# A two-layer hybrid trunk: sixteen row sums spread over two products, parameter products behind x, three inner tiles by block products

## The chip, the core and the metric

The kernel runs on one core of one Trainium2 chip. The metric is the device time of one execution in microseconds (us); less is better. The core has five engines that run their own instruction lists in order and wait for each other through semaphores: TensorE (PE, matrix products, with its weight loads shown as PEld), VectorE (DVE), ScalarE (ACT), GpSimd (POOL) and SyncE (SP). Here SP issues nearly all loads from memory, POOL issues one stream of them, and ACT and DVE prepare operands for PE.

## What is computed

Two pre-norm residual layers over 512 tokens of width 1024, float32. Layer 0 mixes tokens with a state-space layer (S5), layer 1 with forgetting attention (FoX). Each is followed by a gated feed-forward layer (FFN) of inner width 2816 with a causal convolution of width 3. Every sub-layer is modulated by shift, scale and gate, which come from one conditioning vector `c` through a 1024 x 3072 matrix of its own.

```python
def adaln_params(c, w, b):
    mod = jax.nn.silu(c) @ w + b
    shift, scale, gate = jnp.split(mod, 3, axis=-1)
    ...
def s5_mixer(h, w_in, ...):
    u = h @ w_in
    ...                       # discretise, scan over time, read out: y
    y = jax.nn.gelu(y)
    y = y * jax.nn.sigmoid(y @ w_glu)
    return y @ w_out
def conv_ffn(h, w_up, conv_w, conv_b, w_down):
    a, b = jnp.split(h @ w_up, 2, axis=-1)
    ...                       # a_conv: causal convolution of a, width 3
    return (silu(a_conv) * b) @ w_down
for i in range(2):
    h = h + gate * mixer(modulate(h, ...))
    h = h + gate * conv_ffn(modulate(h, ...))
return rmsnorm(h, final_g)
```

## The kernel before

**Products in split form.** Activations lie with features on the 128 partitions and the 512 tokens along the free axis. A product with a weight matrix is made tile by tile: 128 output features (`m`) from 8 input tiles (`k`). To keep float32 precision in PE's faster format, each operand is split in a high and a low part: ACT copies the raw tile to `w_hi` in the rounded format (L277) and DVE subtracts, `w_lo = raw - w_hi` (L278, `put_parts`). PE then does three matmuls for each k (hi by hi, hi by lo, lo by hi, L294). `product` loads a raw tile on SP's queue, has it split, runs its matmuls and calls `evac`, which empties the PSUM tile. There are five buffers each for `w_hi` and `w_lo`, three for `raw`.

**Opening.** The order of the first stage is written by hand (`manual_schedule`). `s5_params` is a generator that makes the S5 parameters out of many small DVE instructions; each `next(params)` emits the piece up to its next `yield`. The piece after the normalisation constants holds `kr`, `ki` and the first two complex products (`cmul` with n = 1 and n = 2, L876 to L881, six DVE instructions each); behind it stands `ga` (L167, the modulation's scale, whose input PE makes at L157 and L162), and behind that the eight instructions that make `x`, one for each k (tile `a_x`, L1130). PE multiplies the first input weight tile by `x` (L1144), two k at a time, between four steps of a product that makes the shift from the weights `ada_w` (L205).

**S5's last two products.** After the scan, `s5` multiplies by `w_glu` (five tiles are done early, into `gps`; three more with `product`) and then by `w_out`. For each tile m of the first product `glu` takes a sigmoid on ACT (L1278), multiplies it on DVE by y, read back from memory (L1279), and splits the result into `zhi` (ACT) and `zlo` (DVE). The product with `w_out` needs `zhi[k]` and `zlo[k]` for k = 0 to 7 in turn, so the eighth tile, made last, is needed at the end of the first `w_out` tile. That tile's evacuation is `h<-mmp` (L362).

**Row sums in the background.** The modulation parameters of later sub-layers are not made on PE but by DVE as row sums: `ada_units` loads 128 rows of 1024 transposed weights into a room `ada_raw` (a DMA that POOL issues, 512 KB, L233), and DVE multiplies them by the row `c_row` and adds them up (L247). A unit is one such row sum; eight units make one shift, scale or gate of a sub-layer, named (i, t). When a unit has been emitted, its room is loaded again for a later one. Units are emitted where a stage calls `tick`:

```python
def tick(self, n):
    while n and self.bg:
        if next(self.bg[0], None) is None:
            self.bg.pop(0)
        else:
            n -= 1
```

The first tick of a list only starts the loads. Eight units, (1, 2), are emitted in the product with `w_out`, two after each tile but the last two; the FFN of layer 0 emits 32 (three parts of sub-layer 2 and (3, 2)).

**The FFN of layer 0.** 22 inner tiles f, in groups of 4, 4, 5, 4 and 5. Each f makes two up tiles (the branch for the convolution and its gate), applies the convolution and silu, and splits the result into `ghi` and `glo`. From the second group on, f is followed by one or two tiles of the down product of the group before. An inner tile is made in one of two ways. A *plain* one is two calls of the usual product: 48 matmuls of 128 x 512. The other way, `quarters`, is by block products: the 2 x 2 blocks of weights and tokens are combined so that seven products of half-size blocks stand for eight: 84 matmuls of 128 x 256 (L550). For this DVE makes four sums of weight blocks (L518, `sums`), splits three tiles of 1024 columns and one of 512 instead of two of 1024, and adds four PSUM pieces (L518, `nm_t`) with copies that ACT makes (L557, `nm_h`). The tuple `plain` names the inner tiles made the first way: 0, 1, 2, 3, 6, 11 and 17.

From f = 4 on the stage ticks once in `gated` and once behind the down tiles, so two units for each f until the list is empty. While units are there, the down weights are loaded into one single room `rawd`, so the next such load can be issued only when DVE has made the `w_lo` of the one before (L278, `w_lo<-rawd`). DVE, ACT and PE instructions of this stage are put in order by the framework's scheduler; the order it makes is part of the program.

**Values of the attention layer.** `fox_values` (L1366) multiplies with the split weights as the moving operand: 96 matmuls with 272 columns and 288 with 256. `VALUES` is the offset, in float32 elements, at which these split weights lie in their buffers; other users of the buffers take 0 or `ASIDE` (22).

## Time and profile before

| what | value |
|---|---|
| median of 3 runs | 1212.27 us |
| lowest and highest | 1211.45 and 1213.45 us |
| the profiled execution | 1215.46 us |
| its span, first to last instruction | 1213.7 us |
| mean granted TensorE clock | 0.991 of full speed |
| ACT busy | 610.0 us, 50% of the span, 1156 instructions |
| POOL busy | 85.8 us, 7%, 145 instructions |
| DMA | 183.81 MB, mean 151 GB/s |

Busy times are of the profiled execution. A busy PE is not a PE at its peak: matmuls overlap, so the time from one to the next is shorter than the duration shown for one. Where a row says "[2.19 <-DVE a_x L1130]", the engine stood idle for 2.19 us before that work, and what ended the wait was the DVE instruction of line 1130 that writes `a_x`.

### The profile page before, as it was taken

What the parts mean: (1) busy time and instruction counts of PE and PEld (TensorE: products, weight loads), DVE (VectorE), ACT (ScalarE), POOL (GpSimd) and SP (SyncE); (2) the same over time, 40 slices, a digit from 0 to 9 for tenths busy, and PEclk for the clock granted to TensorE, in tenths of its full rate; (3) what the DMA queues carried; (4) which work ended last, traced back from release to release, by engine and by line L of the source; (5) the groups of instructions that cost most, each with busy time, mean ns of one, the idle gap of its engine ahead of it and who ended that gap; (6) DMA issues with size and microseconds to landing.
All of it is one profiled execution on the core that took longest, in us unless ns stands there. A gap on an engine that the chain in (4) does not pass through costs nothing.

```text
span 1213.7 us, 20336 instructions
## 1 busy us (share of the span) xinstructions
PE 1183.8 (98%) x7793; PEld 1015.9 (84%) x7793; DVE 1004.6 (83%) x1872; ACT 610.0 (50%) x1156; POOL 85.8 (7%) x145
## 2 busy tenths in 40 slices
PE   6999999999999999999999999999999999999997
PEld 2566678898988899789899888878989999999987
DVE  7799987689899988899788578876899887888865
ACT  3554565335545453445443565764466554555543
POOL 0000000100000000000000343520000000000000
PEclk9899999999999999999999999999999999999999
DMA  9588787531364544544435453432213332333331
GB/s 356 188 266 258 245 271 253 202 99 53 122 204 156 179 163 155 161 159 130 131 125 194 162 173 134 150 109 88 89 55 111 117 121 84 104 103 109 109 100 70
DMA packets 74513, 183.81 MB, mean 151 GB/s; under 512 B 23232, under 2 KB 25632, under 8 KB 73392
## 3 DMA queue, kind: packets, MB, share of 16 engines
q1 hardware_dynamic: 68367, 161.02, 40.5%
q0 software_dynamic: 5760, 20.97, 5.4%
q8 instruction: 61, 1.00, 0.3%
q10 hardware_dynamic: 288, 0.52, 0.1%
q14 instruction: 37, 0.30, 0.1%
HBM read 175.57 MB, written 6.92 MB: 150 GB/s over the span
## 4 chain that ended last, share of the span: by engine, by line
PE 62%; issue 26%; DVE 4%; DMA 4%; POOL 2%; ACT 1%; SPq 0%; POOLq 0%; DVEq 0%; ACTq 0%
PE mmp L294 25%; PE mmp L550 11%; PE aux L550 4%; PE mmp L1174 3%; PE mmp L1366 3%; PE mmp L1203 2%; PE aux L1505 1%; PE aux L1525 1%; POOL ada_raw L233 1%; PE aux L1065 1%; PE mmp L205 1%; DMA ada_raw<-in_ada_t 1%; PE aux L978 1%; PE aux L1057 1%; DVE w_lo L278 1%
## 5 line engine op out<-in xcount | busy, mean ns | idle before, releaser
L278 DVE TENSOR_TENSOR w_lo<-raw,w_hi 128x1024 fp32r<-128x1024 f32 (+4 forms) x173 | 183.2, 1064 | 37.6 <-ACT w_hi L277 37.1
L277 ACT ACTIVATE w_hi<-raw 128x1024 fp32r<-128x1024 f32 (+4 forms) x173 | 154.8, 905 | 102.0 <-PE mmp L294 44.5
L294 PE MATMUL mmp<-ghi,w_hi 128*128 128x512 f32 (+1 forms) x392 | 145.1, 370 | 0.0
L294 PE MATMUL mmp<-ghi,w_lo 128*128 128x512 f32 (+1 forms) x392 | 144.3, 368 | 0.7 <-DVE w_lo L278 0.5
L294 PE MATMUL mmp<-glo,w_hi 128*128 128x512 f32 (+1 forms) x392 | 144.6, 369 | 0.0
L294 PE MATMUL mmp<-a_hi,w_hi 128*128 128x512 f32 (+1 forms) x376 | 138.4, 371 | 1.5 <-ACT a_hi L433 1.5
L294 PE MATMUL mmp<-a_hi,w_lo 128*128 128x512 f32 (+1 forms) x376 | 136.1, 362 | 0.3 <-DVE w_lo L278 0.3
L294 PE MATMUL mmp<-a_lo,w_hi 128*128 128x512 f32 (+1 forms) x376 | 135.7, 362 | 0.0
L550 PE MATMUL mmp<-w_hi 128*128 128x256 f32 x396 | 109.9, 278 | 3.0 <-ACT nm_h L557 2.5
L550 PE MATMUL mmp<-w_hi,w_lo 128*128 128x256 f32 x396 | 109.7, 278 | 0.7 <-DVE w_lo L278 0.7
L550 PE MATMUL mmp<-w_lo,w_hi 128*128 128x256 f32 x396 | 109.5, 277 | 0.0
L557 ACT ACTIVATE nm_h<-mmp 128x256 f32<-128x256 f32 x99 | 37.2, 381 | 108.3 <-PE mmp L550 108.3
L278 DVE TENSOR_TENSOR w_lo<-sums,w_hi 128x1024 fp32r<-128x1024 f32 x74 | 90.1, 1220 | 0.0
L277 ACT ACTIVATE w_hi<-sums 128x1024 fp32r<-128x1024 f32 x74 | 77.0, 1054 | 25.3 <-DVE sums L518 23.4
L294 PEld LDWEIGHTS mmp<-ghi,w_lo 128*128 128x128 f32 x392 | 74.2, 189 | 13.9 <-DVE w_lo L278 1.4
L294 PEld LDWEIGHTS mmp<-ghi,w_hi 128*128 128x128 f32 x392 | 74.2, 189 | 11.9 <-ACT w_hi L277 0.6
L294 PEld LDWEIGHTS mmp<-glo,w_hi 128*128 128x128 f32 x392 | 74.2, 189 | 11.0
L294 PEld LDWEIGHTS mmp<-a_hi,w_hi 128*128 128x128 f32 x376 | 70.2, 188 | 13.2 <-ACT a_hi L433 1.9
L294 PEld LDWEIGHTS mmp<-a_hi,w_lo 128*128 128x128 f32 x376 | 70.6, 188 | 12.5 <-DVE w_lo L278 1.3
L294 PEld LDWEIGHTS mmp<-a_lo,w_hi 128*128 128x128 f32 x376 | 70.7, 188 | 9.7
L362 DVE SCALAR_TENSOR_TENSOR h<-mmp,par,h 128x512 f32<-128x512 f32 (+1 forms) x100 | 68.1, 683 | 11.8 <-PE mmp L294 11.6
L550 PEld LDWEIGHTS mmp<-w_hi 128*128 128x128 f32 x396 | 74.5, 188 | 3.6 <-ACT nm_h L557 2.9
(319 smaller groups left out, 3082.2 us busy)
## 6 DMA issues: line engine op xcount, KB each, us to landing
raw<-in_w_up SPq DMA_DIRECT2D x88, 512.0 KB, 3.4
raw<-in_ada_w SPq DMA_DIRECT2D x40, 512.0 KB, 6.4
ada_raw<-in_ada_t POOLq DMA_DIRECT2D x40, 512.0 KB, 3.9
nf<-nfd SPq DMA_DIRECT2D x8, 1152.0 KB, 7.8
raw<-in_fox_qk SPq DMA_DIRECT2D x16, 512.0 KB, 3.6
raw<-in_w_down SPq DMA_DIRECT2D x24, 320.0 KB, 3.2
rawd<-in_w_down SPq DMA_DIRECT2D x24, 256.0 KB, 3.3
raw<-in_w_down SPq DMA_DIRECT2D x16, 384.0 KB, 3.4
```

The lines of the kernel that those rows point to most:

```text
L205: self.last_mm = nc.tensor.matmul(ps[32 * qq:32 * qq + 32, :], self.sc32[:, k, :], w[:, q * S:(q + 1) * S], start=(step is steps[0]), stop ...
L233: (nc.gpsimd if late else nc.sync).dma_start(ws[n], src)
L277: nc.scalar.activation(hi, src, AF.Copy)
L278: return nc.vector.tensor_tensor(lo, src, hi.bitcast(F32), ALU.subtract)
L294: self.last_mm = self.nc.tensor.matmul(o, wt, xt[:, cols], start=(k == 0 and n == 0), stop=(k == nk - 1 and n == 2),)
L362: add = self.nc.vector.scalar_tensor_tensor(self.h[:, m, cols], ps, self.par[i][:, 16 + m:17 + m], self.h[:, m, cols], op0=ALU.mult, op1=A ...
L550: self.last_mm = nc.tensor.matmul(o, wt[:, k], xt[:, k], start=(first and k == 0 and n == 0), stop=(k == H - 1 and n == 2), skip_group_che ...
L557: a = nc.scalar.activation(t, o, AF.Copy)
L978: nc.tensor.matmul(ps[:, :, cols], x[:, q, r].rearrange("p c j -> p (c j)"), both[:, :, planes, q, :], start=(r == 0), stop=(r == 1), skip ...
L1174: nc.tensor.matmul(ps, w[m][:, k, :], x[:, k], start=(k == 0), stop=(k == KT - 1))
L1203: nc.tensor.matmul(gps[m], wt, xt[:, k], start=(k == 0 and part == 0 and xt is yhi), stop=(k == KT - 1 and part == 1))
L1366: self.last_mm = nc.tensor.matmul(ps[q, b][:, :n], xt[:, k, tb], wt, start=(k == 0 and i == 0), stop=(k == KT - 1 and i == 2),)
```

## The change

Four edits stand in the diff.

1. `fox_values` puts its split weights at offset 16 instead of 106.
2. `s5_params` yields at two more places, behind `ki` and ahead of the product with n = 2, and the loop that makes `x` takes one piece after its third and one after its sixth tile. The first two complex products are so emitted between the tiles of `x`.
3. The list of units in S5's last two products is longer by the eight of (3, 2), sixteen in all, and has three rooms. It ticks once ahead of the three remaining `w_glu` tiles and then in the products themselves, at every fourth k of both, in place of two ticks after a `w_out` tile. The FFN of layer 0 has 24 units instead of 32.
4. In the FFN of layer 0 the inner tiles 6, 11 and 17 are made by block products.

```diff
+import itertools
...
-ROOM, ASIDE, VALUES = 9 * P, 22, P - 22
+ROOM, ASIDE, VALUES = 9 * P, 22, 16
...
         ki = e.mul(ki, rd, keep("ki"))
+        yield
         w1 = tp.tile([P, L, H], F32, name="s5_w1")
...
         for n in (1, 2, 4):
-            if n == 4:
+            if n > 1:
                 yield
...
                             x[:, k], self.h[:, k], self.ga[i][:, k:k + 1], rb, op0=ALU.mult, op1=ALU.mult
                         )
+                        if k in (2, 5):
+                            next(params)
...
-            self.bg = [self.ada_units(units((1, 2)), rooms=("ada_raw", "ada_raw2"))]
+            self.bg = [self.ada_units(units((1, 2), (3, 2)), rooms=("ada_raw", "ada_raw2", "ada_raw3"))]
+            turn = itertools.count(1)
+
+            def step():
+                if next(turn) % 4 == 0:
+                    self.tick(1)
+
             for m in range(HEAD + 1):
                 glu(m, gps[m], slice(0, S))
-            self.product(self.io["s5_w_glu"], range(HEAD + 1, KT), KT, (yhi, ylo), glu)
             self.tick(1)
+            self.product(self.io["s5_w_glu"], range(HEAD + 1, KT), KT, (yhi, ylo), glu, step=step)
             after, y = nxt
             self.product(
-                self.io["s5_w_out"], range(KT), KT, (zhi, zlo), self.add_residual(i), tail=2, after=after, ticks=2
+                self.io["s5_w_out"], range(KT), KT, (zhi, zlo), self.add_residual(i), tail=2, after=after, step=step
             )
...
-        k.bg = [k.ada_units(units(*((2, t) for t in range(3)), (3, 2)))]
-        x = k.ffn(1, 0, x, k.norm_mod(2), ticks=1, plain=(0, 1, 2, 3, 6, 11, 17))
+        k.bg = [k.ada_units(units(*((2, t) for t in range(3))))]
+        x = k.ffn(1, 0, x, k.norm_mod(2), ticks=1, plain=(0, 1, 2, 3))
```

Three places in DVE's list show what moves. Line numbers of the changed kernel are a few higher.

The opening, DVE, before: the last rows of the complex product with n = 2 (`s_w`, `s_pr`, `s_pi`), then `ga`, then all of `x`.

```order
L878 TENSOR_TENSOR s_pr<-s_w_369,s_w_370 128x2x32
L879 TENSOR_TENSOR s_w_369<-s_pr,s_pi 128x64
L880 TENSOR_TENSOR s_w_370<-s_pi,s_pr 128x64
L881 TENSOR_TENSOR s_pi<-s_w_369,s_w_370 128x2x32
L167 SCALAR_TENSOR_TENSOR ga_96<-aux,rest 128x8
L1130 SCALAR_TENSOR_TENSOR a_x<-h,ga_96,aux 128x512 x8
L876 TENSOR_TENSOR s_w_369<-s_pr 128x128
```

The same place of the changed kernel:

```order
L702 TENSOR_TENSOR s_ki<-s_ring_180 128x32
L168 SCALAR_TENSOR_TENSOR ga_96<-aux,rest 128x8
L1132 SCALAR_TENSOR_TENSOR a_x<-h,ga_96,aux 128x512 x3
L878 TENSOR_TENSOR s_w_381<-s_pr 128x32
L879 TENSOR_TENSOR s_w_382<-s_pi 128x32
L880 TENSOR_TENSOR s_pr<-s_w_381,s_w_382 128x32
L881 TENSOR_TENSOR s_w_381<-s_pr,s_pi 128x32
L882 TENSOR_TENSOR s_w_382<-s_pi,s_pr 128x32
L883 TENSOR_TENSOR s_pi<-s_w_381,s_w_382 128x32
L1132 SCALAR_TENSOR_TENSOR a_x<-h,ga_96,aux 128x512 x3
```

Twelve small instructions that stood ahead of `ga` and `x` now stand between the tiles of `x`, six after the third and six after the sixth.

The end of the product with `w_glu`, DVE, before: `w_lo` are split weights for the tiles to come, `nm_t<-nm_t,yt` is the multiplication by y, and the last three rows are the eighth tile of z and the evacuation of the first `w_out` tile.

```order
L278 TENSOR_TENSOR w_lo<-raw,w_hi 128x1024
L1279 TENSOR_TENSOR nm_t<-nm_t,yt 128x8x64
L278 TENSOR_TENSOR zlo<-nm_t,zhi 128x512
L278 TENSOR_TENSOR w_lo<-raw,w_hi 128x1024
L1279 TENSOR_TENSOR nm_t<-nm_t,yt 128x8x64
L278 TENSOR_TENSOR zlo<-nm_t,zhi 128x512
L362 SCALAR_TENSOR_TENSOR h<-mmp,par_92,h 128x512
```

The same place of the changed kernel, from the last two row sums ahead of the eighth tile on:

```order
L248 ISA ada_raw,ada_s<-ada_raw,c_row 128x1024
L248 ISA ada_s 128x1
L248 ISA ada_raw_2090,ada_s<-ada_raw_2090,c_row 128x1024
L248 ISA ada_s 128x1
L279 TENSOR_TENSOR w_lo<-raw,w_hi 128x1024
L1283 TENSOR_TENSOR nm_t<-nm_t,yt 128x8x64
L255 TENSOR_TENSOR par_93<-ada_s,rest 128x8
L279 TENSOR_TENSOR w_lo<-raw,w_hi 128x1024
L279 TENSOR_TENSOR zlo<-nm_t,zhi 128x512
L279 TENSOR_TENSOR w_lo<-raw,w_hi 128x1024 x2
L1283 TENSOR_TENSOR nm_t<-nm_t,yt 128x8x64
L279 TENSOR_TENSOR zlo<-nm_t,zhi 128x512
```

Of the eight row sums that now stand ahead of the first `h<-mmp`, three come before the first multiplication by y and five between the tiles of z; the last two splits of weights, which before stood on both sides of the seventh tile's `zlo`, now follow each other ahead of the eighth.

In the FFN of layer 0, the fourth group, DVE, before: from one use of the single room `rawd` to the next.

```order
L278 TENSOR_TENSOR w_lo<-rawd,w_hi 128x640
L518 TENSOR_TENSOR sums<-raw 128x512 x2
L518 TENSOR_TENSOR nm_t<-aux,nm_h 128x256
L518 TENSOR_TENSOR sums<-sums,raw 128x512
L518 TENSOR_TENSOR sums<-raw,sums 128x512
L518 TENSOR_TENSOR nm_t<-mmp,nm_h 128x256
L278 TENSOR_TENSOR w_lo<-rawd,w_hi 128x640
```

The same place of the changed kernel:

```order
L279 TENSOR_TENSOR w_lo<-rawd,w_hi 128x640
L519 TENSOR_TENSOR sums<-raw 128x512 x2
L519 TENSOR_TENSOR sums<-sums,raw 128x512
L519 TENSOR_TENSOR nm_t<-mmp,nm_h 128x256
L519 TENSOR_TENSOR sums<-raw,sums 128x512
L603 SCALAR_TENSOR_TENSOR conv<-nm_t,conv_wb,conv 128x511
L279 TENSOR_TENSOR w_lo<-raw,w_hi 128x512
L603 SCALAR_TENSOR_TENSOR conv<-nm_t,conv_wb,conv 128x510
L248 ISA ada_raw,ada_s<-ada_raw,c_row 128x1024
L248 ISA ada_s 128x1
L519 TENSOR_TENSOR nm_t<-mmp,nm_h 128x256 x2
L279 TENSOR_TENSOR w_lo<-rawd,w_hi 128x640
```

The scheduler has put the two convolution steps, a split, a row sum and two additions between the two uses of the room, where before the second use followed directly.

## The prediction

> **What bounds the kernel now.** The page's first part and the head of its chain come first; columns are busy time, share of the span and instructions.
>
> ```profile
> PE 1183.8 (98%) x7793; PEld 1015.9 (84%) x7793; DVE 1004.6 (83%) x1872; ACT 610.0 (50%) x1156; POOL 85.8 (7%) x145
> ...
> PE 62%; issue 26%; DVE 4%; DMA 4%; POOL 2%; ACT 1%; SPq 0%; POOLq 0%; DVEq 0%; ACTq 0%
> ```
>
> PE sets the time: its own work and its issue make 88% of the chain. DVE is the one engine near it. So an edit can gain by fewer matmuls or by shorter waits of PE, and it can lose by making DVE late. The view of waits (engine, line, for whom: total us, times, longest) names PE's waits; each starts where DVE or ACT is late.
>
> ```profile
> PE mmp L550 <- ACT nm_h L557: 2.5, 1, 2.5
> PE mmp L1144 <- DVE a_x L1130: 2.2, 1, 2.2
> ...
> PE mmp L550 <- DVE w_lo L278: 1.6, 2, 0.9
> ```
>
> These totals are small because records of matmuls overlap. What a matmul really takes is read in the chain's pieces (start, us, what) where PE runs freely, in the second FFN.
>
> ```profile
> 951.57 8.18 PE mmp L294 x36
> ...
> 962.49 1.36 PE aux L550 x12
> ```
>
> 8.18 / 36 = 0.227 us for 512 columns, 1.36 / 12 = 0.113 for 256. With these I count out the first FFN in three stretches: inner tiles 4 to 12, 13 to 16 and 17 to 21 (up to the last down product). The windows give for each: length, busy us of PE, PEld, DVE, ACT and POOL with their instructions, clock, DMA share, GB/s.
>
> ```profile
> 305.29:439.63 134.34, 133.55 (x876) 121.07 (x875) 123.52 (x194) 65.99 (x106) 8.45 (x16) 1.00 0.53 170
> 439.63:507.87 68.24, 66.52 (x458) 60.74 (x457) 56.18 (x89) 30.69 (x51) 4.24 (x8) 1.00 0.44 145
> 507.87:579.21 71.34, 68.00 (x457) 62.33 (x456) 64.67 (x100) 32.50 (x54) 3.69 (x7) 0.98 0.47 151
> 351.51:405.56 54.05, 53.26 (x398) 49.76 (x396) 51.29 (x82) 27.41 (x46) 3.70 (x7) 1.00 0.51 167
> ```
>
> The 876 matmuls of the first are 588 of 256 columns (7 block tiles) and 288 of 512 (2 plain tiles, 16 down tiles): 588 x 0.1135 + 288 x 0.2272 = 132.2 us, so PE lost **2.2**. In the second, 336 and 120 make 65.4: lost **2.8**. In the third, 336 and 120 again: lost **5.9**. These 10.9 us and the matmuls themselves are what the change can win here.
>
> **The change, part by part. Three block tiles.** PE: a plain tile is 48 x 0.2272 = 10.9 us, a block tile 84 x 0.1135 = 9.5. Three of them: **-4.1**, two in the first stretch, one in the third. DVE pays; its price from one start to the next is read where two equal instructions stand together (start, us, engine, line, operation, tiles):
>
> ```profile
> 298.92 2.35 DVE L278 TENSOR_TENSOR w_lo<-raw,w_hi 128x1024 fp32r<-128x1024 f32 x2
> ...
> 315.22 0.75 DVE L518 TENSOR_TENSOR nm_t<-mmp,nm_h 128x256 f32<-128x256 f32 x2
> ...
> 339.67 1.29 DVE L518 TENSOR_TENSOR sums<-raw 128x512 f32<-128x512 f32 x2
> ```
>
> A second one adds 1.14, 0.33 and 0.60 us. A block tile needs 4 sums of blocks (2.4), one split of 1024 more (1.14), one of 512 (0.6) and 4 additions (1.3) more than a plain one: 5.5 us. In all a block tile is 10.3 us of DVE: sums 2.4, splits 3 x 1.14 + 0.6, additions 1.3, and 2.5 for the four instructions of 512 columns (two convolution steps, the gate, `glo`) that a plain tile has too; a plain tile is 4.8, a down tile 1.3 (a split and `h`), a row sum 1.14. Tiles 4 to 12 with 16 down tiles and 17 row sums are then 121 us (the window shows 123.5 busy, ends of instructions included) and go to 132, while PE's falls to 129.4. DVE becomes the longer one by 2.8 us over nine tiles. The fourth window shows such a stretch: tiles 7 to 10, all by blocks, hold 55.5 us of DVE work by the same prices against 51.8 of PE, an excess of 3.7, and PE lost 2.2 there; 1.5 was carried by work made ahead or left for later, in the plain tiles 6 and 11. Of an excess of 2.8, 1.3 would be left; for waits of DVE itself I add 1.7 and take 3.0 lost after (2.2 before).
>
> **Eight row sums fewer in this FFN.** The list now ends with tile 16, so one row sum of 1.14 us leaves the second stretch and seven, 8 us, the third. The third's DVE work is 64.7 - 8 + 5.5 = 62.2 busy against PE's 64.0, the second's 55 against 65.4. What loses time there, though, is the single room `rawd`: the tile view shows who waited for its load, and two rows show one place.
>
> ```profile
>   ACT w_hi L277: 33.0, 14
>   DVE w_lo L278: 13.5, 7
> ...
> 527.90 0.63 ACT L277 ACTIVATE w_hi<-rawd 128x512 fp32r<-128x512 f32 x1 [3.57 <-DMA rawd<-in_w_down]
> 528.44 0.64 ACT L557 ACTIVATE nm_h<-mmp 128x256 f32<-128x256 f32 x2
> ```
>
> ACT stands 3.57 us for the load, and behind it in ACT's list stand the copies for which PE waits its 2.5 us. It comes when two uses of the room lie close on DVE. By the prices above the work between the uses of one tile was 3.1, 3.1, 3.1 and 0.7 us in tiles 13 to 16, and is 5.3, 5.9, 6.5 and 3.1 now; in the last group two pairs stay at 2.8. So I take 1.0 lost in the second stretch (2.8 before) and 2.0 in the third (5.9). Losses together 6.0 instead of 10.9: **-4.9**. The ends of what is lost: 1.3 (DVE's excess alone) and 19 (with the second rival below).
>
> **Row sums in S5's last products.** Sixteen sums instead of eight; eight stand ahead of the first `w_out` evacuation.
>
> ```profile
> 179.59 0.47 SPq L1270 DMA_DIRECT2D c_row<-scd  x1
> ...
> 183.74 1.18 DVE L1192 TENSOR_TENSOR a_lo<-yt,a_hi 128x512 fp32r<-128x512 f32 x1 [0.83 <-ACT a_hi L1191]
> 190.44 1.23 DVE L278 TENSOR_TENSOR w_lo<-raw,w_hi 128x1024 fp32r<-128x1024 f32 x1 [5.52 <-ACT w_hi L277]
> ...
> 214.22 1.23 DVE L278 TENSOR_TENSOR w_lo<-raw,w_hi 128x1024 fp32r<-128x1024 f32 x1 [1.73 <-ACT w_hi L277]
> 215.36 1.16 DVE L1279 TENSOR_TENSOR nm_t<-nm_t,yt 128x512 f32<-128x512 f32 x1
> 217.22 0.69 DVE L278 TENSOR_TENSOR zlo<-nm_t,zhi 128x512 fp32r<-128x512 f32 x1 [0.70 <-ACT zhi L277]
> 218.82 0.75 DVE L362 SCALAR_TENSOR_TENSOR h<-mmp,par,h 128x512 f32<-128x512 f32 x1 [0.90 <-PE mmp L294]
> ...
> 190.44:214.22 23.78, 23.78 (x111) 19.86 (x110) 20.23 (x23) 14.89 (x23) 0.00 (x0) 1.00 0.72 223
> ...
> DMA to landing us min/median/max: 6.7/6.7/6.7
> ```
>
> Three sums fall in DVE's gap of 5.52 us: `c_row` is there at 179.6 + 6.7 = 186.3 (the landing row is its own), three times 1.14 end at 189.7, and the next split starts at 190.4 as before. The other five, 5.7 us, join 20.2 us of work in 23.8: they need 25.9, so what started at 214.22 starts 2.2 later, and the eighth tile of z with it. PE used that tile within 0.3 us of its being made (`zlo` ends at 217.9, three matmuls of 0.227 end the tile at 218.8). Cost **+1.9**; behind the waiting matmul stand all later ones, so nothing hides it. Ends: 0, if the sums fall in the waits for `zhi` too, and +5.7, if no gap serves. The eight sums behind it stood there before too, with two rooms and waits for their loads; three rooms can only shorten these, and PE did not wait there: 0. POOL issues nothing else there; SP keeps its loads' kinds and count.
>
> **Parameters behind x.**
>
> ```profile
> 19.47 0.37 SPq L186 DMA_DIRECT2D raw<-in_s_w_in  x1
> ...
> 22.54 1.03 PE L162 MATMUL aux<-sel,ada_rows 128*128 128x2 f32 x8
> 27.03 2.71 PE L1144 MATMUL mmp<-a_x,raw 128*128 128x512 f32 x4 [2.19 <-DVE a_x L1130]
> ...
> 26.04 0.16 DVE L167 SCALAR_TENSOR_TENSOR ga<-aux,rest 128x8 f32<-128x8 f32 x1
> ...
> DMA to landing us min/median/max: 5.5/7.9/10.2
> ...
> 43.36 9.55 PE mmp L1174 x16
> 52.91 2.19 PE aux L978 x16
> ```
>
> `ga` could run when PE ends L162, at 23.6; twelve small instructions hold it until 26.0. Now it goes at once, 2.4 us earlier. The first input weights land at 19.47 + 5.5 = 25.0 (the landing row is of the two `s_w_in` loads), so PE starts at 25.0 instead of 27.03: **-2.0**. The later tiles of `x` come 1.3 us apart from the small products, still ahead of PE's pairs. From there to 55 the chain is PE's own work but for 0.2 us, and the scan's first products follow it, so I keep all of it. Ends: 0, if a load or DVE takes it back, and -2.4, all by which `ga` is earlier.
>
> **The offset of the values.**
>
> ```profile
> 641.87 23.93 PE mmp L1366 x198
> ...
> 959.75 2.74 PE mmp L550 x24
> ```
>
> At offset 106 a 256-column matmul of `fox_values` takes 0.121 us, elsewhere 0.114. No trace shows offset 16. Over 288 matmuls the ends are -2.1 (as elsewhere) and +2.1 (as far the other way). This is the one 256-column kind off the common row, so I take half the way to it: **-1.0**.
>
> **Sum.** -4.1 - 4.9 + 1.9 - 2.0 - 1.0 = -10.1. The profiled execution took 1215.5 us around its span of 1213.7, which makes 1205.4; the median of the runs shown lies 3.2 below that execution: 1212.3 - 10.1 = **1202.2 us**.
>
> **Rivals.**
> *The losses in the FFN stay.* DVE's excess early takes the place of the waits on `rawd`. For it: ACT still waits in order for that room. Against: the longer distances. The 4.9 fall away: 1207.1.
> *DVE becomes the bound, and it gets slower.* In tiles 4 to 12 each block tile with two row sums needs 15.1 us of DVE (10.3, two down tiles 2.5, sums 2.3) where PE needs 9.5 + 5.5 = 15.0; with one down tile 13.8 against 12.3. DVE then has no spare for any wait of its own. In the third stretch it was busy 64.7 of 71.3, 91%; at that share 132 us need 145.6 instead of my 132.4, 13.2 more: 1215.4. It decides from the point where DVE's own waits in these nine tiles pass the 3 us that I allow. Against: the fourth window, where DVE was busy 51.3 of 54.05, 95%, and PE lost 2.2.
> *The sums come on the path in S5.* Loads of the rooms run late and DVE stands in front of the splits: +5.7 instead of 1.9 is 1206.0. The Trainium skill, "Trainium Kernel Development and Optimization", section Key Constraints, says that DMAs issued from SP, ACT and POOL queues run on the same 16 DMA engines and interleave; by it SP's weight loads give way to POOL's eight more. The window above has those engines at 0.72.
> *The clock.* The wait before 27.03 goes, and with it perhaps the slow clock behind it:
>
> ```profile
> 27.03:30.20 3.17, 3.17 (x8) 0.88 (x12) 3.17 (x6) 0.00 (x0) 0.00 (x0) 0.68 1.03 420
> ```
>
> Granted 0.68 of full, 3.17 us lose 1.0; with later dips perhaps 2 more: 1199. The Trainium skill, "TensorE: Matmul & The Clock Gate", section What's actually happening, has PE's clock fall to half after an idle window of about 3.4 us, in windows that run free of the kernel; the dip behind a wait of 2.2 us and little work agrees as far as it goes.
>
> **How the numbers follow.** Forecast 42 in 100; losses stay 14; sums on the path 11; clock 7; the second and third together, about 1211, 10; DVE the bound 16, of which 2 within the bounds of no change. About 0.2%, 2.4 us, is what a measurement of this kernel can tell from no change. Faster 0.42 + 0.14 + 0.11 + 0.07 = 0.74, same 0.12, slower 0.14. The range takes the clock's case and the best ends of the offset and the FFN below, 1196, and the two rivals together with the offset's bad end above, 1213.5; it leaves out DVE as the bound and a little below.
>
> **What would show it.** Right: `ga` near 23.7 and PE's first L1144 near 25.0; a wait of PE for `zhi` or `zlo` of about 2 us near the first `w_out` tile; tiles 4 to 12 in 132 to 133 us, 13 to 16 in 66 to 67, 17 to 21 in 66; L1366 at 0.114 to 0.121 us. Wrong: tiles 4 to 12 at 140 or more with DVE at 97%; `w_hi<-rawd` still waiting 3 us ahead of `nm_h`; L1174 ending where it did, at 52.9.

## The result, and the profile after

The change makes the kernel slower. The median of five runs is 1226.4 us (1223.1 to 1230.1) against 1212.8 us (1211.5 to 1215.8) for the kernel before, timed alongside it; the ratio is 1.0109, with a 95% interval of 1.0084 to 1.0134. The profiled execution spans 1222.0 us, 8.3 more than the one before; it is one of the faster ones of the changed kernel, and the one before is among the slower of its kind, so the profiles show a smaller difference than the medians. The last section comes back to a part of this.

The page of the changed kernel, first part (busy time, share of the span, instructions) and head of the chain that ended last:

```profile
PE 1183.5 (97%) x7901; PEld 1018.8 (83%) x7901; DVE 1022.3 (84%) x1902; ACT 618.7 (51%) x1174; POOL 86.3 (7%) x145
...
PE 66%; DVE 14%; DMA 9%; issue 7%; ACT 2%; SPq 0%; POOL 0%; DVEq 0%; ACTq 0%; POOLq 0%
```

PE is as busy as before, but DVE's share of the chain is 14% where it was 4%, and DMA's 9% where it was 4%. So work of DVE and loads now stand on the path. The view of PE's waits (engine, line, for whom: total us, times, longest) says where:

```profile
PE mmp L295 <- ACT zhi L278: 5.7, 1, 5.7
...
PE mmp L295 <- DVE w_lo L279: 5.1, 6, 1.8
PE aux L381 <- DVE ssq L357: 3.8, 2, 3.5
PE mmp L295 <- ACT w_hi L278: 2.1, 1, 2.1
```

The first row is one wait, in S5's last products, and there was none for `zhi` before. The second and fourth are down products of the first FFN. The windows (length, busy us of PE, PEld, DVE, ACT and POOL with their instructions, clock, DMA share, GB/s) give the stages: first the stretch from the start of `w_glu` to the first FFN's norm before, then the same after, then the three stretches of the first FFN after.

```profile
195.69:255.63 59.94, 59.69 (x309) 51.00 (x308) 44.95 (x69) 23.32 (x33) 3.69 (x7) 1.00 0.60 197
```

```profile
189.80:257.67 67.87, 61.90 (x309) 51.95 (x308) 51.81 (x82) 24.42 (x34) 5.81 (x11) 0.95 0.61 213
...
307.61:444.71 137.10, 132.69 (x939) 121.66 (x937) 127.73 (x202) 68.16 (x114) 7.93 (x15) 0.99 0.48 156
444.71:520.99 76.28, 71.32 (x467) 64.10 (x467) 67.88 (x108) 35.72 (x57) 4.22 (x8) 0.98 0.47 156
520.99:585.12 64.13, 64.13 (x493) 61.23 (x492) 56.40 (x87) 34.48 (x59) 0.00 (x0) 1.00 0.33 96
```

| stretch | before, us | after, us | difference | predicted |
|---|---|---|---|---|
| start to S5's scan (first product L978, now L980) | 52.75 | 46.25 | -6.5 | -2.0 |
| scan, to `w_glu` | 142.9 | 143.5 | +0.6 | 0 |
| `w_glu` and `w_out`, to the norm | 59.9 | 67.9 | +7.9 | +1.9 |
| norm, and inner tiles 0 to 3 | 49.7 | 49.9 | +0.3 | 0 |
| inner tiles 4 to 12 | 134.3 | 137.1 | +2.8 | -1.9 |
| 13 to 16 | 68.2 | 76.3 | +8.0 | -1.8 |
| 17 to 21 | 71.3 | 64.1 | -7.2 | -5.3 |
| the last down products, to `fox_values` | 38.1 | 41.3 | +3.2 | 0 |
| `fox_values` | 48.4 | 47.6 | -0.8 | -1.0 |
| the rest | 537.7 | 537.7 | 0.0 | 0 |

Three places lose: S5's last products, the middle of the FFN, and the FFN's end.

**S5's last products.** The chain of work that ended last, in order of time (start, us, what), runs there through four engines and one load:

```profile
205.08 1.21 DVE ada_raw L248
...
206.31 1.14 DVE ada_raw L248
...
207.45 1.15 DVE w_lo L279
...
208.65 5.30 DMA raw<-in_s_w_out
...
214.03 1.06 ACT w_hi L278
...
216.26 1.08 DVE nm_t L1283
...
217.37 0.64 ACT zhi L278
...
218.05 4.15 PE mmp L295 x9
```

Two row sums stand ahead of a `w_lo`. That `w_lo` frees a room of raw weights, so SP can issue the next load only at 208.65. The load takes 5.30 us. ACT's row for its copy shows how it waits for such loads, and what stands behind the copy:

```profile
209.24 1.06 ACT L278 ACTIVATE w_hi<-raw 128x1024 fp32r<-128x1024 f32 x1 [4.66 <-DMA raw<-in_s_w_out]
...
214.03 1.06 ACT L278 ACTIVATE w_hi<-raw 128x1024 fp32r<-128x1024 f32 x1 [3.21 <-DMA raw<-in_s_w_out]
214.99 0.58 ACT L1282 ACTIVATE nm_t<-mmp 128x512 f32<-128x512 f32 x1
```

The row at 214.99 is the sigmoid of the eighth tile. Its input was ready long before, but it is behind `w_hi` in ACT's list, and `w_hi` is of a weight tile that PE needs only later. PE stands 5.7 us for the eighth `zhi`, and its granted clock (the last figure but two) is at about half when it goes on:

```profile
218.05:221.81 3.76, 3.76 (x9) 2.70 (x10) 2.44 (x3) 1.69 (x2) 0.00 (x0) 0.52 0.25 101
```

3.76 us at 0.52 lose 1.8, so the wait and the slow clock behind it make 7.5 of the 7.9 us.

**The first FFN.** DVE's waits in tiles 13 to 17, by line, then two rows of its timeline:

```profile
DVE sums L519 <- DMA raw<-in_w_up: 4.4, 2, 2.3
DVE w_lo L279 <- ACT w_hi L278: 1.5, 1, 1.5
```

```profile
440.51 0.69 DVE L519 TENSOR_TENSOR sums<-raw 128x512 f32<-128x512 f32 x1 [2.06 <-DMA raw<-in_w_up]
...
458.63 0.69 DVE L519 TENSOR_TENSOR sums<-raw 128x512 f32<-128x512 f32 x1 [2.26 <-DMA raw<-in_w_up]
```

In the kernel before DVE never waited for a load of `w_up` in these tiles: it made `sums` and splits ahead, and its waits were for ACT. SP's issues of the two loads of a tile (start, us from the first to the end of the second), before and after, show what changed:

```profile
451.26 10.03 SPq L186 DMA_DIRECT2D raw<-in_w_up  x2
```

```profile
435.56 0.90 SPq L187 DMA_DIRECT2D raw<-in_w_up  x2
```

Before, the first load went out 10.0 us ahead of the second in two of the pairs between 400 and 490 us, and 1.4 to 7.6 us ahead in the other three; after, four of five pairs went out within 0.9 us. The waits of SP's queue in tiles 4 to 16 name what it stood for, after and then before:

```profile
SPq L187 <- DVE sums L519: 44.3, 7, 9.1
```

```profile
SPq L186 <- DVE sums L518: 4.5, 1, 4.5
```

Now DVE reads the raw tiles for `sums` so late that SP issues both loads together, and DVE stands over 2 us for them three times, at 440, 458 and 476 us. The engine that is late makes its own next wait.

### The profile page after: what moved, and what is told of

Same layout as the page of the kernel before. It is cut to its first block, busy times and chain, and to the rows that moved or that the text cites. A ratio compares the mean times of both kernels' runs of the same rounds, so it can differ in the third digit from the quotient of the medians.

```text
span 1222.0 us, 20601 instructions
## 1 busy us (share of the span) xinstructions
PE 1183.5 (97%) x7901; PEld 1018.8 (83%) x7901; DVE 1022.3 (84%) x1902; ACT 618.7 (51%) x1174; POOL 86.3 (7%) x145
## 4 chain that ended last, share of the span: by engine, by line
PE 66%; DVE 14%; DMA 9%; issue 7%; ACT 2%; SPq 0%; POOL 0%; DVEq 0%; ACTq 0%; POOLq 0%
PE mmp L295 33%; PE mmp L551 13%; PE aux L551 5%; DVE w_lo L279 3%; PE mmp L1178 3%; PE mmp L1376 2%; PE aux L1515 1%; PE aux L1535 1%; DVE ada_raw L248 1%; DMA raw<-in_w_up 1%; DMA rawd<-in_w_down 1%; DMA raw<-in_s_w_glu 1%; DVE sums L519 1%; PE aux L1059 1%; PE aux L980 1%
## 5 line engine op out<-in xcount | busy, mean ns | idle before, releaser
L295 PE MATMUL mmp<-a_hi,w_hi 128*128 128x512 f32 (+1 forms) x328 | 119.9, 369 | 1.5 <-ACT a_hi L434 1.5
L551 PE MATMUL mmp<-w_hi 128*128 128x256 f32 x432 | 119.6, 277 | 1.2 <-ACT w_hi L278 1.0
L551 PE MATMUL mmp<-w_hi,w_lo 128*128 128x256 f32 x432 | 119.1, 277 | 0.4 <-DVE w_lo L279 0.4
L551 PE MATMUL mmp<-w_lo,w_hi 128*128 128x256 f32 x432 | 119.3, 276 | 0.0
L295 PE MATMUL mmp<-a_hi,w_lo 128*128 128x512 f32 (+1 forms) x328 | 117.6, 359 | 0.0
L295 PE MATMUL mmp<-a_lo,w_hi 128*128 128x512 f32 (+1 forms) x328 | 117.3, 359 | 0.0
L279 DVE TENSOR_TENSOR w_lo<-sums,w_hi 128x1024 fp32r<-128x1024 f32 x80 | 97.4, 1220 | 0.2 <-ACT w_hi L278 0.2
L551 PEld LDWEIGHTS mmp<-w_hi,w_lo 128*128 128x128 f32 x432 | 80.9, 188 | 0.9 <-DVE w_lo L279 0.7
L551 PEld LDWEIGHTS mmp<-w_lo,w_hi 128*128 128x128 f32 x432 | 81.1, 188 | 0.0
L551 PE MATMUL mmp<-a_hi,w_lo 128*128 128x256 f32 x288 | 80.4, 279 | 0.6 <-DVE w_lo L279 0.5
```

The lines of the kernel that those rows point to most:

```text
L279: return nc.vector.tensor_tensor(lo, src, hi.bitcast(F32), ALU.subtract)
L295: self.last_mm = self.nc.tensor.matmul(o, wt, xt[:, cols], start=(k == 0 and n == 0), stop=(k == nk - 1 and n == 2),)
L551: self.last_mm = nc.tensor.matmul(o, wt[:, k], xt[:, k], start=(first and k == 0 and n == 0), stop=(k == H - 1 and n == 2), skip_group_che ...
```

## The experiments

Ratios are of the runs of each kernel to runs of the kernel before on the same chip, with 95% intervals. "The S5 stretch" is the one from `w_glu` to the norm (59.9 us before, 67.9 after); "the FFN stretch" is inner tiles 4 to 21 (273.9 before, 277.5 after; their matmuls alone, at 0.2272 and 0.1135 us each, take 263.0 before and 258.8 after).

### One edit undone, or alone

The moved row sums undone:

```diff
-units((1, 2), (3, 2)), rooms=("ada_raw", "ada_raw2", "ada_raw3")
+units((1, 2)), rooms=("ada_raw", "ada_raw2")
...
-tail=2, after=after, step=step
+tail=2, after=after, ticks=2
...
-units(*((2, t) for t in range(3)))
+units(*((2, t) for t in range(3)), (3, 2))
```

> The changed kernel with the sixteen row sums put back where they were: eight in S5's last product, 32 in the first FFN (offset, opening and three block tiles stay). Theory (each edit pays by its own stage): the stretch from the start of w_glu to the first FFN's norm, 67.9 us in the changed kernel and 59.9 before, is back at 60; tiles 4 to 21 of the first FFN, 277.5 us in the changed kernel, get eight row sums (9.1 us of DVE) more while DVE is already the late engine, so 283 to 287; total 1226.4 - 7.9 + 5 to 9 = 1224 to 1228. Rival (the FFN's stalls come from S5's delay being carried on, not from the blocks): tiles 4 to 21 fall to about 267, total near 1208.

Measured: 1215.9 us, ratio 1.0026 (1.0009 to 1.0043). The S5 stretch is back at 59.9. The FFN stretch is 280.4, 3 more than in the changed kernel. So the moved sums cost 8 us where they went and gave back 3 where they came from. The total is 8 us under the 1224 to 1228 that I expected: tiles 4 to 21 lost less than the 5 to 9 us that I had put down, and the stretch behind them took 36.2 us instead of 41.3.

The three block tiles undone:

```diff
-x = k.ffn(1, 0, x, k.norm_mod(2), ticks=1, plain=(0, 1, 2, 3))
+x = k.ffn(1, 0, x, k.norm_mod(2), ticks=1, plain=(0, 1, 2, 3, 6, 11, 17))
```

> The changed kernel with tiles 6, 11 and 17 as plain products again (offset, opening and moved row sums stay). Theory (the blocks put DVE behind its loads in the first FFN): tiles 4 to 21 go from 277.5 to 264 to 268 us (their matmuls alone need 263), the S5 stretch stays at 67 to 68, total 1226.4 - 10 to 13 = 1213 to 1217, no change against before. Rival (the moved sums' loads and SP's order make the stalls, the blocks only shift them): tiles 4 to 21 stay at 274 or more, total 1223 or more.

Measured: 1215.9 us, ratio 1.0041 (1.0021 to 1.0061). The FFN stretch falls to 270.5 us, not to the 264 to 268 that I expected, and the S5 stretch is 70.4. Either edit without the other still makes a kernel slower than the one before, by 0.3 to 0.4%.

The opening alone, and the opening with the offset, on the kernel before (the diffs are the first lines of the change's):

> The kernel before with the parameter products behind x alone. Theory (the wait of 2.2 us at the first input product and the half clock behind it are one loss): first scan product near 46 to 47 us instead of 52.75, total 1212.5 - 5 to 6.5 = 1206 to 1207.5. As predicted at first, without the clock: -2.0, 1210.5. Rival (the start of the program differed by chance and DVE takes the rest back in the scan): 1212.

> The kernel before with the parameter products behind x and the offset 16 of the values. Theory: 288 matmuls at 0.117 instead of 0.120 us, 0.8 us less than with the opening alone, 1205 to 1207. Rival (the pitch follows the clock, not the offset): the same time as with the opening alone and a pitch of 0.120.

Measured: 1210.2 us, 0.9985 (0.9968 to 1.0003), and 1208.9 us, 0.9985 (0.9967 to 1.0004). My expectation of -5 to -6.5 us was wrong. The first, -2.0, lies in the interval, and so does no change. The trace shows its mechanism: with the opening alone PE's first input product starts at 24.9 instead of 27.0. Most of the 6.5 us between the two profiles was not won by this edit; the last section comes back to it. The offset moves the middle of the matmul's pitch in `fox_values` from 0.120 us to 0.118, which is 0.6 us over 288 matmuls. The times don't separate it.

### What the row sums cost in S5: VectorE's time or their loads

Two kernels, each the changed one with one half left out in S5's list alone. In the first, the sums after the third run over rooms already loaded, so thirteen loads are left out:

```diff
+                if not loads and n >= len(rooms):
+                    ws[n] = kept[n % len(rooms)]
+                    return
```

> The changed kernel; in S5's list of sixteen row sums the first three rooms are loaded and every later sum is taken over a room already loaded, so thirteen of POOL's sixteen loads there are left out (and with them part of the conditioning's values). Stretch from w_glu's start to the first FFN's norm: 67.9 us in the changed kernel, 59.9 before. Theory A (VectorE's 1.2 us per sum in front of the weight splits is the cost): stays at 66 to 68. Theory B (POOL's loads slow the weights' loads on the shared DMA engines, and ACT stands for them): falls to 60 to 62. Both half: 63 to 65.

In the second, all loads stay and a sum has 16 columns, `full` being false for this list:

```diff
+                cols_ = D if full else 16
...
-                    w, w, self.c_row, 1.0, 0.0, ALU.mult, ALU.add, sums[:, j:j + 1]
+                    w[:, :cols_], w[:, :cols_], self.c_row[:, :cols_], 1.0, 0.0, ALU.mult, ALU.add, sums[:, j:j + 1]
```

> The changed kernel; in S5's list each of the sixteen row sums runs over 16 columns instead of 1024 (the rest of each sum is left out), while all sixteen loads stay. Same stretch: Theory A (VectorE's time): falls to 60 to 62. Theory B (the loads): stays at 66 to 68. Both half: 63 to 65.

Measured: 1218.9 us, 1.0058 (1.0025 to 1.0090), without the loads, and 1224.1 us, 1.0103 (1.0065 to 1.0141), with the loads and hardly any sums. The windows of the S5 stretch, the kernel with sums and no loads first, then the one with loads and hardly any sums:

```profile
190.55:252.80 62.25, 60.21 (x310) 50.95 (x308) 50.23 (x80) 23.36 (x33) 0.00 (x0) 1.00 0.41 135
```

```profile
189.20:256.20 67.00, 63.26 (x310) 52.62 (x308) 40.36 (x82) 25.71 (x36) 5.25 (x10) 0.95 0.61 217
```

DVE's time alone costs 62.2 - 59.9 = 2.3 us, close to the 1.9 that I had put down. The loads alone cost 7.1 us, with DVE only 40 us busy: there PE stands 3.5 us for `zhi` and `zlo`, and its clock is 0.50 from 215.6 to 221.2, which loses 2.8 more. In the full change sums and loads together cost 7.9, not 9.4: the two overlap. So without the loads most of the loss is gone.

How do they cost it? The view of DMA issues (KB each, median us from issue to landing) shows the weights' loads between 195 and 222 us in the kernel before, then in the one with the loads, and between 195 and 218 us in the changed kernel:

```profile
raw<-in_s_w_out SPq DMA_DIRECT2D x7, 512.0 KB, 4.6
```

```profile
ada_raw<-in_ada_t POOLq DMA_DIRECT2D x6, 512.0 KB, 6.6
raw<-in_s_w_out SPq DMA_DIRECT2D x5, 512.0 KB, 7.4
```

```profile
raw<-in_s_w_out SPq DMA_DIRECT2D x6, 512.0 KB, 4.3
```

The Trainium skill, "DMA: Bandwidth & Descriptors", section Issuing engines are not separate DMA queues, says that loads issued from different engines run on the same 16 DMA engines and interleave. 7.4 us instead of 4.6 in the kernel with the loads agrees. But these slower loads are not what PE waited for: ACT stands only 1.2 us for these loads there, and in the changed kernel their median is no longer than before. What stands on the path is single loads. In the kernel with the loads and hardly any sums the chain goes through a row sum's load and, later, through one of y:

```profile
181.04 5.68 DMA ada_raw<-in_ada_t
...
201.29 8.50 DMA yt<-s_yd
```

Loads of y took 3.6 us on the median before. The row sum's load shows as a wait of DVE in list order, from 180 to 222 us of the same kernel (total, times, longest); the wait of 5.8 us is ahead of the first multiplication by y:

```profile
DVE ada_raw L249 <- DMA ada_raw<-in_ada_t: 6.9, 2, 5.8
```

In the changed kernel the load on the chain is the fifth of `w_out`. Without POOL's loads it goes out 16.3 us into the stretch and takes 3.5 us; in the changed kernel it goes out at 18.9 and takes 5.3. So the loads cost by a later issue, behind a later DVE, and by one slower landing; the runs don't divide the loss further.

### The sums later: all sixteen in `w_out`

If the loads of `w_glu` were what they collide with, it would help to emit them after it. Kernel before, with opening and offset, and:

```diff
-units((1, 2)), rooms=("ada_raw", "ada_raw2")
+units((1, 2), (3, 2)), rooms=("ada_raw", "ada_raw2")
...
-tail=2, after=after, ticks=2
+tail=2, after=after, ticks=3
```

(and (3, 2) taken from the FFN's list).

> The kernel before with the parameter products behind x, the offset 16, and all sixteen row sums of S5's list in the w_out product (three per tile, two rooms, none during w_glu); the first FFN has 24. Theory B (in w_glu the sums' loads meet the weights' loads; in w_out the weights are loaded ahead): the stretch from w_glu's start to the norm stays at 60 to 62 us, the FFN's tiles gain 3 us as in no_blocks, total 1209 - 1 to 3 = 1206 to 1208. Rival (anywhere in S5 the sums are on the path): the stretch takes 65 or more, total 1212 or more.

Measured: 1222.1 us, 1.0070 (1.0045 to 1.0095). A miss. The eighth tile of z is in time now, but PE waits at the norm behind `w_out`. Its waits in this kernel:

```profile
PE aux L380 <- DVE ssq L356: 7.3, 3, 5.1
...
PE aux L410 <- DVE rs_y L401: 4.8, 3, 4.4
```

The S5 stretch is 74.2 us. DVE waits 0.2 to 0.8 us for the load of nearly each sum, and the sums of squares for the norm stand behind them. With two rooms for the down weights and tile 17 by block products added, it stays there: 1220.6 us, 1.0063 (1.0038 to 1.0088), more than 10 us above either range that I had put down.

> late_sums with two rooms for the down weights and tile 17 by block products: both gains of the two theories together, 1209 - 2 - 6 - 1.4, 1198 to 1203. If the sums are on the path in w_out: 1204 to 1210.

So neither place in these products had 9 us to spare.

### The single room for down weights

The changed kernel with two rooms, and to make place for the second an unused stretch of memory in this stage, the filler, 128 bytes shorter:

```diff
-            t = self.bgpool.tile(shape, F32, name=self.room, bufs=1)
+            t = self.bgpool.tile(shape, F32, name=self.room, bufs=2)
```

> The changed kernel with two rooms for the down weights in the first FFN instead of one (128 bytes less of the filler there). Tiles 4 to 21 took 277.5 us in the changed kernel, their matmuls 259. Theory C (the single room: SyncE stands in its list until VectorE frees it, so the next loads of w_up come late and two at once): VectorE's waits for w_up's loads (7.0 us in 4 times) go and the stretch falls to 264 to 268, total 1226.4 - 10 = 1216. Theory D (the three rooms of w_up's weights, freed late by VectorE, are the limit): 274 or more, total 1223 or more.

Measured: 1217.1 us, 1.0063 (1.0033 to 1.0093); the FFN stretch is 272.8, not the 264 to 268 expected. DVE's waits for `w_up` fall from 7.0 to 3.3 us. ACT no longer waits for `rawd`. But a block tile where PE runs freely takes 9.83 us here instead of 9.54, for a reason found below.

Four rooms for raw weights instead of three:

> The changed kernel with four rooms for raw weights instead of three (in both FFNs and everywhere else; the filler in the FFNs is 64 bytes instead of 1696). Theory D (three rooms are the limit in the first FFN): tiles 4 to 21 fall from 277.5 to 264 to 268 us, and ACT's waits for w_out's weights in S5 shrink, so that stretch falls from 67.9 to 62 to 65; total 1226.4 - 12 to 16 = 1210 to 1214. Theory C (the single down room) or E (VectorE's amount of work alone, 252 us of it in 277): 274 or more in the FFN.

Measured: 1236.7 us, 1.0212 (1.0175 to 1.0250), 10 us worse than the change. The FFN stretch is some 280 us, not the 264 to 268 of theory D. It tells little of rooms, since the shorter filler moved the tiles of both FFNs: in the second FFN, where nothing waits, 24 matmuls of 256 columns take 2.82 us, against 2.72 in the changed kernel. DVE's waits for `w_up` are gone in the first FFN, as theory D has it, but the time is not; the S5 stretch, 66.3, hardly moved.

Two rooms on the kernel before with opening and offset, its 32 sums and plain tiles kept; and the same with tile 17 by block products:

> The kernel before with the parameter products behind x, the offset 16 and two rooms for the down weights in the first FFN; its 32 row sums and plain tiles stay. Theory C (the single room is what made the stalls of the kernel before too): tiles 4 to 21 fall from 274 us towards their matmuls' 263, by 4 to 8 us, total 1209 - 4 to 8 = 1201 to 1205. Rival (the second room only helps where VectorE is overloaded by blocks): no change against 1209.

> As open_off_rawd2, and tile 17 by block products (6 and 11 stay plain). Theory (there VectorE is not late, so the block's 1.4 us of TensorE are won): 1.4 us under open_off_rawd2. Rival (32 row sums plus a block put VectorE behind at 17 as well): 1 to 3 us over it.

Measured: 1204.8 us, 0.9927 (0.9904 to 0.9950), and 1207.7 us, 0.9956 (0.9939 to 0.9972). In the first PE has no gap above 0.4 us left between tile 4 and tile 21, so nearly all of the 10.9 us that the kernel before lost there was the room's. One block tile more costs 2.9 us where its matmuls are 1.4 us shorter.

### The pitch, and the blocks and sums apart

The filler shortened by 512 bytes instead of 128, first on the kernel with opening, offset and two rooms, then with the three block tiles, then with the whole change:

```diff
-            fill(pool, 1696 - (128 if ticks else 0))
+            fill(pool, 1696 - (512 if ticks else 0))
```

> open_off_rawd2 with the filler of the first FFN shortened by 512 bytes instead of 128. Theory F (the place of the moving operand in steps of 512 bytes sets the matmul's pitch): a block tile is back from 9.83 to 9.54 us, a down tile of 24 matmuls from 5.60 to 5.47, 4 to 21 in 264 to 265 instead of 269; total 1204.8 - 4 to 5 = 1200 to 1201. Rival (the pitch has another reason): 9.83 stays, 1204 to 1206.

> open_off_rawd2_512 with tiles 6, 11 and 17 by block products. Theory G (with two rooms VectorE's amount of work still binds: 32 row sums and three blocks more are 16.5 us more than in the kernel before): 2 to 6 us slower than open_off_rawd2_512, VectorE over 96% busy from tile 6 on, TensorE waiting for w_lo<-sums. Theory H (the rooms were all of it): 3 to 4 us faster, as the matmuls' count says.

> The whole change with two rooms for the down weights and the filler 512 bytes shorter. By theories B and G: S5's stretch 67 to 70 us (8 to 10 more than before), the FFN's tiles 4 to 21 in 262 to 266 with eight row sums fewer than in three_blocks_rawd2_512; total about 1212 to 1216, level with the kernel before. Rival (what S5 loses the FFN regains): within 2 us of three_blocks_rawd2_512 and under 1206.

One block tile without a wait, with 128 and then with 512 bytes:

```profile
453.28:463.11 9.83, 9.83 (x86) 9.83 (x84) 8.81 (x14) 5.06 (x9) 0.53 (x1) 1.00 0.52 180
```

```profile
451.97:461.51 9.54, 9.54 (x86) 9.54 (x84) 9.32 (x15) 4.99 (x8) 0.53 (x1) 1.00 0.56 187
```

Measured: 1199.7 us, 0.9883 (0.9861 to 0.9905), the fastest kernel of the study; 1207.9 us, 0.9954 (0.9936 to 0.9973), with the three block tiles; 1216.2 us, 1.0025 (1.0005 to 1.0046), with the moved sums too. The blocks cost 8.2 us, more than the 2 to 6 that I expected, and the sums 8.3, with two rooms and an undisturbed pitch (the time from one matmul to the next); with the whole change the S5 stretch takes 68.8 us and the FFN stretch 270.3. The FFN stretch of the first two:

```profile
302.85:566.51 263.66, 263.38 (x1789) 242.35 (x1787) 244.75 (x383) 132.43 (x210) 16.38 (x31) 1.00 0.50 165
```

```profile
299.11:572.61 273.50, 265.77 (x1896) 247.70 (x1895) 260.43 (x412) 139.75 (x228) 16.37 (x31) 0.99 0.47 158
```

In the first, PE's matmuls need 263.0 us and take 263.7: nothing is left to win there by waits. DVE has 244.8 us of work, 93%. The blocks add 15.7 us to DVE, 260.4, more than the 258.8 that PE's matmuls now need. So DVE is the longer one, and its own waits come on top. In the worst tiles of this kernel it works nearly all the time:

```profile
400.02:417.50 17.48, 15.22 (x106) 13.85 (x105) 17.05 (x29) 8.05 (x15) 1.58 (x3) 1.00 0.46 155
...
405.26 0.39 PE L550 MATMUL mmp<-w_hi,w_lo 128*128 128x256 f32 x1 [2.10 <-DVE w_lo L278]
```

17.05 of 17.48 us, and PE waits 2.1 us for a split of `sums`.

## Why the prediction was wrong

**What bounds the kernel** was read rightly, and the prediction named DVE as the one engine near the bound. Two of its terms then took from DVE's reserve, and both were too small.

**Row sums in S5 (+1.9 predicted, +7.9).** The step that failed is "POOL issues nothing else there; SP keeps its loads' kinds and count". It counted DVE's time, and there the working holds: sums without loads cost 2.3. It gave the eight earlier loads no price. Leaving out the loads takes the cost from 7.9 to 2.3; loads with hardly any sums cost 7.1. The rival for this place named loads that run late and DVE in front of the splits, and gave it 5.7 us; that was again DVE's time, with the time of a load left out. SP's giving way to POOL in general is not shown: the median landing of the weights' loads stayed (4.3 us against 4.6), and one load went out later and landed later. PE's wait for `zhi` appeared where the prediction said, 5.7 us instead of 2, and the half clock behind it, 1.8 us, was in no term.

**Losses in the FFN (6.0 us predicted, 18.7 in the profile).** The step that failed is "for waits of DVE itself I add 1.7 and take 3.0 lost after". The fourth window, by which I took 3.0, is a stretch of four block tiles between two plain ones, 6 and 11, in which by my count DVE caught up; the change takes just these away, so an excess is carried from tile to tile. That this is why the window misled is argued, not tested. The prices of DVE's instructions were right: 15.7 us for three blocks, where 3 x 5.5 = 16.5 was predicted. What the excess turns into was wrong. DVE did not merely end 2.8 us late; it lost its lead over its loads, and stood over 2 us for `w_up` three times. The rival of DVE as the bound gave this with the right trigger, DVE's own waits passing 3 us (5.4 us for loads alone in tiles 4 to 12): in tiles 4 to 16 it had 145.6 + 66.4 = 212.0 us, and the profile shows 213.4, with the loss later than the rival put it. It had 16 in 100.

**Eight row sums fewer in the FFN (-4.9).** The gain came, though smaller: with the blocks undone, the FFN stretch falls from 273.9 to 270.5, and in the changed kernel tiles 17 to 21 take 64.1 where 66 was predicted. The longer distances between the uses of `rawd` are not shown to be the reason: with the blocks undone ACT stands 41.1 us for its loads instead of 33.0, and what fell is PE's longest wait for `nm_h`, from 2.5 us to 1.0. The waits on `rawd` have a plainer cure: the second room takes all of them.

**Three block tiles (-4.1).** By the count PE's matmuls did shrink by 4.1 us. The net is a loss, 8.2 us in the cleanest comparison.

**Parameters behind x (-2.0).** Right in mechanism: `ga` runs at 24.3 instead of 26.0, the first input product at 25.3. Alone it is 0.9 us faster by the medians and 1.8 by the ratio, with an interval that holds both -2.0 and no change. The slow clock that the clock's rival saw behind this wait did go, from 0.69 to 1.00 between 27 and 30 us.

**Offset (-1.0).** The pitch went from 0.120 to 0.117 us, `fox_values` is 0.8 us shorter in the profile.

**The end of the FFN (0 predicted, +3.2)** was not in the sum. PE waits 3.5 us instead of 1.6 for `ssq`, and the clock behind it is 0.50 for 6.1 us. By the same ends the stretch takes 35.6 to 36.1 us in the kernels with two rooms, but also 36.2 in the one with the sums undone, which has one. So the single room alone does not explain it, and the cause stays open.

**The range** ended at 1213.5, because it left out DVE as the bound and took the S5 rival with its price. Both came true together. The ends that it names don't quite add up to its bounds, either: by the terms given they make about 1193 and 1214.

## What to carry to other kernels

When one engine has a few per cent to spare against another, don't price new work for it by duration: ask whether it stays ahead of its own loads, since an engine that falls behind frees its rooms late, and each load then stands open on the path. A piece of background work that brings a load can cost an in-order wait and make a load beside it late, even where its engine time is hidden; price the load too. Look for a room that serializes before adding faster arithmetic: one more buffer of 2.5 KB per partition brought 9.2 us here by the medians, about as much as all four edits were expected to.

## What the runs showed of the hardware that was not expected

**The place of tiles moves PE's pitch.** With the filler shortened by 128 bytes, a free block tile of 84 matmuls took 9.83 us, with 512 bytes 9.54: 3%, and 5 us over the kernel. Which operand's place counts, and which other shifts keep the pitch, was not tried.

**Half the clock comes and goes, with and without a wait.** Behind PE's waits of 5.7 and 2.1 us in the changed kernel its clock was at half: 0.52 over 3.8 us in the window above, and behind the shorter one

```profile
426.57:429.82 3.25, 3.25 (x11) 2.61 (x12) 3.25 (x5) 1.41 (x2) 0.53 (x1) 0.50 0.49 159
```

The Trainium skill, "TensorE: Matmul & The Clock Gate", section What's actually happening, puts an idle window of about 3.4 us before it; a wait of 2.1 us was enough here. Each slow stretch inside the two profiles lasts 3.4 or 6.8 us (426.4 to 429.9 and 214.8 to 221.6 in the changed kernel, for example), so that a wait of 2 us can cost 1.7 us more. But there is also a dip early in S5 that follows no such wait: PE's gaps ahead of it are 0.3 us. Just ahead of it PE makes 16 matmuls of a single column, in 2.0 to 2.5 us, but so it does in the changed kernel, where there is no dip. These windows are of the kernel before, of the opening alone, of the changed kernel, and of the one with the sums undone, in which the dip lies 30 us later:

```profile
43.15:48.27 5.12, 5.12 (x7) 2.03 (x7) 4.98 (x10) 5.04 (x10) 0.00 (x0) 0.50 0.60 192
```

```profile
40.62:45.74 5.12, 5.12 (x8) 2.02 (x7) 5.05 (x9) 5.05 (x10) 0.00 (x0) 0.50 0.59 199
```

```profile
39.30:46.25 6.95, 6.95 (x19) 2.95 (x17) 6.74 (x15) 6.78 (x15) 0.00 (x0) 1.00 0.72 226
```

```profile
72.62:77.62 5.00, 5.00 (x8) 2.18 (x7) 5.00 (x7) 0.83 (x3) 0.00 (x0) 0.50 0.76 196
```

The kernel with opening and offset has the same opening as the one with the opening alone, and no dip there: its clock is 1.00 from 40 to 47 us. So whether the dip falls into an execution, and where, is not set by the edits. In the kernel before the clock is 0.50 from 41.8 to 48.6 us, which loses 3.4 of the 6.5 us that the opening seems to gain between the two profiles; the earlier dip, from 28.2 to 31.6 us behind PE's wait, loses 1.7. Two profiles alone would have credited all of it to the edit; the times of many runs did not. What sets the later dip off stays open.
